# A transformer layer on one core: attention weights formed with the keys on partitions

## The chip, the cores and the metric

The kernel runs on one core of a Trainium2 chip. The metric is the device time in microseconds (us). Before the change it was 1210.74 us, the median of three runs (1210.34 to 1212.61). The engines are PE (TensorE, matrix products), DVE (VectorE), ACT (ScalarE) and POOL (GpSimd); SP is the queue that issues nearly all the loads.

## The reference

One layer over 256 latent tokens and 256 context tokens of width 1024:

```python
mod = jnp.split((silu_c @ w_ada[l] + b_ada[l])[:, None, :], 6, axis=-1)
h = modulate(rms_norm(x, g_mix_pre[l]), mod[0], mod[1])      # and hc from ctx
y, yc = token_mixing(h, hc, ...)        # attention, then @ w_o
x = x + mod[2] * rms_norm(y, g_mix_post[l])
h2 = modulate(rms_norm(x, g_ffn_pre[l]), mod[3], mod[4])
f = moe_ffn(h2, ...)                    # top 4 of 32 experts, swiglu
x = x + mod[5] * rms_norm(f, g_ffn_post[l])
```

`token_mixing` has two groups of eight heads. The first (GQA, heads of 64, two key heads) reads all context keys and the latent keys within 128 positions; its softmax has one more logit per head, the sink, which adds to the sum and has no value. The second (MLA) has queries and keys of 96 (64 and 32) and values of 64, formed by two further projections. Each softmax runs over 512 keys, and the 16 head outputs of 64 columns are multiplied by `w_o`.

## The kernel before

Everything that must be exact to fp32 is computed on PE in one of two ways: natively (an fp32 product), or as `mm3` (L137 to L139): both operands are split into a high and a low part of the type fp32r (L128 copies the high part on ACT, L129 subtracts on DVE or POOL), and three fp32r products are added in PSUM.

The program has three parts. First, up to about 98 us, the modulation rows, the norms and the projections into `qTg`, `kTg`, `vg` (GQA) and the latent vectors (MLA). Second, attention: 16 heads go through a loop of 19 steps. In step u head u gets its scores for the two query tiles (`scores`: an `mm3` of 128 queries by 512 keys, for GQA a mask product, then the row maximum on DVE at L614, the negated maximum at L616 or L619, the exponential with its row sum on ACT at L628, the sink's term at L634, the reciprocal at L636 and the scaling of the weights at L637, on POOL for query tile 0 and on DVE for 1). Head u-2 gets its weights transposed, 128 by 128 at a time (`flip_p`, L646), and split; head u-3 its values (`values`, L656: high and low parts of the values lie side by side in 128 columns, so the result is two halves that are added at L669). Two heads make one of eight blocks of the output product, `mix` (L677 natively for blocks 0 to 3, `mm3` for 4 to 7, with the weights `wo` split into two parts).

Between these steps stand jobs that don't belong to attention: `k_up`, `q_up`, `v_up` form the MLA keys, queries and values; `ada_load` loads four modulation rows, 1 MB for every quarter of a row, into buffers of a ring (`slot`), and `ada_do` multiplies and adds each quarter with two DVE instructions on 128x1024 (L427; two of the rows have every second one on ACT and POOL, L424 and L425). The last row goes into `vpost`. `spread1` and `column` bring the rows into the shape in which they are used.

Third, from `mix(7)` on: `y` is normed, the router picks experts, and 32 experts are computed from 384 loads of 1 MB each (`wexp`, L744), 18 buffers in turn: eight of the ring, six that are free once attention is over, four of a second ring. L926 are the experts' products.

A scheduler sets the order of PE, DVE, ACT and POOL up to `mix(7)`; on SP the order is that of the program, as it is for all engines afterwards. Each engine executes its list strictly in order.

Of the kernel before, what the change touches and what calls it, by code (L numbers as in the profile page):

```python
# [69 lines left out]
WOU = (3, 6, 9, 12)  # L70
# [3 lines left out]
def layer_kernel(ctx, tc, x, cx, cc, wadr, bada, grows, win0, winB, winC, winD, wuqa, wuqb, wukv, wo, wr, wexp, bgu, bgx, bdn, cols, rows, consts, out):  # L74
# [7 lines left out]
    def slot():  # L82
        return ring.tile([P, 2048], F32, name="slot", tag="slot")

# [89 lines left out]
    pq.tile([P, 512], F32, name="p", tag="pb")  # L174
# [151 lines left out]
    def halves(n):  # L326
        r = slot().bitcast(F32R)
        return [r[:, i * n:(i + 1) * n] for i in range(2048 // n)]

    ckvT = [x_.rearrange("p (i k c) -> p i k c", k=2, c=P) for x_ in halves(1024)]  # L330
    kv_ = slot().bitcast(F32R)
    kTg = [kv_[:, 0:512], kv_[:, 512:1024]]
    vg = kv_[:, 1024:2048].rearrange("p (i h c) -> p i h c", h=2, c=P)
    qTg = [x_.rearrange("p (t j c) -> p t j c", t=NT, c=P) for x_ in halves(1024)]
# [39 lines left out]
    def stage_b(i, p_):  # L374
        t = i - 2
        pv = p_[:, 128:256].rearrange("p (h d) -> p h d", h=2)
        S.copy(vg[:, i, :, 0:64], pv)
        V.tensor_tensor(vg[:, i, :, 64:128], pv, vg.bitcast(F32)[:, i, :, 0:64], op=ALU.subtract)
# [99 lines left out]
    vm = av.tile([P, 4, 8, P], F32R, name="vm")  # L478
    nsink = sm.tile([P, 8], F32, name="nsink", bufs=1)
    V.tensor_scalar(nsink, row[:, 0, R_SINK:R_SINK + 8], -1.0, None, op0=ALU.mult)  # L480
    pslot = slot()
# [37 lines left out]
    def v_up(i):  # L519
        pv = up(i, prow(), wv).rearrange("p (h d) -> p h d", h=8)  # L520
        S.copy(vm[:, i, :, 0:64], pv)
        V.tensor_tensor(vm[:, i, :, 64:128], pv, vm.bitcast(F32)[:, i, :, 0:64], op=ALU.subtract)

    prep = {0: [(k_up, 0), (k_up, 1)], 1: [(k_up, 2), (k_up, 3)], 2: [(q_up, 0, 0), (q_up, 0, 1)],
            3: [(v_split,), (q_up, 1, 0), (q_up, 1, 1)], 4: [(v_up, 0), (v_up, 1)], 5: [(v_up, 2), (v_up, 3)]}
# [10 lines left out]
    wos = {}  # L536

    def load_wo(i):
        wos[i] = slot()
        nc.sync.dma_start(wos[i], wo[i])  # L540

    def split_wo(i, qs):
        w = wos[i]
        if i in NATWO:
            for k in range(2):
                wov[2 * i + k] = w[:, k * 1024:(k + 1) * 1024]
            return
        if qs[0] == 0:
            wos[i, 0] = slot().bitcast(F32R), slot().bitcast(F32R)
        hi, lo = wos[i, 0]  # L550
        for q in qs:
            sl = slice(q * 512, (q + 1) * 512)
            split(hi[:, sl], lo[:, sl], w[:, sl], eng=G if q % 2 else V)
        for k in range(2):
            wov[2 * i + k] = [x_[:, k * 1024:(k + 1) * 1024] for x_ in (hi, lo)]
# [8 lines left out]
    def spread0(ch):  # L564
        gs_[ch] = gs, hl = slot(), slot().bitcast(F32R)
        q = 0 if ch == 0 else 1
        S.dma_start(gs[:, 0:D], bass.AP(tensor=grows.tensor, offset=grows.offset + q * D, ap=[[0, P], [1, D]]))
        for q in range(2):
            sl = slice(q * 512, (q + 1) * 512)
            split(hl[:, sl], hl[:, D + q * 512:D + (q + 1) * 512], accs[ch][:, sl], eng=G)  # L570

    def spread1(ch):
        a, (gs, hl) = accs[ch], gs_[ch]
        for n in range(2):
            sl = slice(n * 512, (n + 1) * 512)
            p_ = pmm((P, 512))
            PE.matmul(p_, onesr, hl[:, sl], start=True, stop=False)
            PE.matmul(p_, onesr, hl[:, D + n * 512:D + (n + 1) * 512], start=False, stop=True)
# [104 lines left out]
    def side(u):  # L683
# [5 lines left out]
        if 0 <= u < 12:  # L689
            ada_do()  # L690
# [566 lines left out]
```

## Time and profile before

| | |
|---|---|
| median of three runs | 1210.74 us |
| the profiled execution's own time | 1209.01 us |
| its span, first to last instruction | 1207.2 us |
| PE busy | 1108.8 us (92%) |
| DVE, ACT, POOL busy | 339.1, 277.1, 152.2 us |
| granted TensorE clock, mean | 0.975 |
| chain that ended last, by engine | DMA 54%, PE 34%, DVE 8% |
| moved by DMA | 446.59 MB, 370 GB/s on average |

The chain that ended last is followed back from the last instruction; its shares say on what the end waited, not what was busy. A row "start, us, ... xN" is a stretch of N records of one kind. Matrix products overlap: the time that one takes from the next is the distance of their starts (the pitch), not the duration shown. A native fp32 product leaves two records, an fp32r product one.

### The profile page before, as it was taken

To read this page: it belongs to the slowest core of one execution; us is meant where nothing else is said; L and a number is where in the kernel's file an instruction comes from. 1 tells how busy PE (TensorE), PEld (TensorE's weight loads), DVE (VectorE), ACT (ScalarE), POOL (GpSimd) and SP (SyncE) were. 2 spreads that over 40 slices of the span, in tenths; PEclk is the share of its full clock that TensorE was granted. 3 is DMA by queue.
4 is the path that set the end of the run, shared out by engine and by line. 5 is a ranking of instruction groups with operands and counts; after the bars stand their busy time and mean duration, and the time that the engine had idled before them with its cause. 6 is when DMAs were issued, how large, how long until landed. Compare 5 with 4: busy or idle time off the path is not lost.

```text
span 1207.2 us, 13663 instructions
## 1 busy us (share of the span) xinstructions
PE 1108.8 (92%) x5321; PEld 484.0 (40%) x5321; DVE 339.1 (28%) x778; ACT 277.1 (23%) x623; POOL 152.2 (13%) x182
## 2 busy tenths in 40 slices
PE   7798888999999999999989899989899999999985
PEld 1596556863433434343333333333333333333321
DVE  3867997752111111111111111111111111111112
ACT  4445654641111111111101111111111111111101
POOL 0503533310011010101010000000000101010000
PEclk9999879999999999999999999999999999999998
DMA  9534461699999999999999999999999999999994
GB/s 381 223 149 175 150 252 53 258 412 422 376 421 421 420 420 420 420 420 421 421 420 420 421 420 420 421 420 420 420 420 421 422 420 420 421 420 421 421 422 172
DMA packets 63196, 446.59 MB, mean 370 GB/s; under 512 B 7284, under 2 KB 7540, under 8 KB 10008
## 3 DMA queue, kind: packets, MB, share of 16 engines
q1 hardware_dynamic: 62648, 444.23, 89.4%
q10 hardware_dynamic: 480, 1.44, 0.3%
q8 instruction: 44, 0.72, 0.2%
q14 instruction: 24, 0.20, 0.0%
HBM read 444.60 MB, written 1.05 MB: 369 GB/s over the span
## 4 chain that ended last, share of the span: by engine, by line
DMA 54%; PE 34%; DVE 8%; ACT 1%; issue 1%; POOL 0%; SPq 0%; POOLq 0%; DVEq 0%; ACTq 0%
DMA slot<-in_wexp 53%; PE pw L926 19%; PE px L891 2%; PE mm L267 2%; PE acc L956 2%; DVE accw L427 1%; PE mm L137 1%; PE y L677 1%; PE pf L939 1%; PE mm L139 1%; PE mm L138 1%; PE mm L656 1%; DVE mx L614 1%; PE mm L646 1%; DVE accw L314 1%
## 5 line engine op out<-in xcount | busy, mean ns | idle before, releaser
L926 PE MATMUL pw<-slot,xg 128*64 128x512 f32 x2048 | 468.0, 598 | 19.3 <-DMA slot<-in_wexp 19.2
L926 PE MATMUL pw<-slot,actT 128*64 128x512 f32 x1024 | 242.8, 600 | 28.3 <-DMA slot<-in_wexp 26.9
L926 PEld LDWEIGHTS pw<-slot,xg 128*64 128x64 f32 x2048 | 136.5, 136 | 302.5 <-issue 233.2
L944 DVE TENSOR_TENSOR z<-pf,bg 128x512 f32<-128x512 f32 x64 | 44.3, 692 | 754.3 <-PE pf L939 754.3
L926 PEld LDWEIGHTS pw<-slot,actT 128*64 128x64 f32 x1024 | 68.6, 136 | 178.5 <-issue 101.5
L948 ACT ACTIVATE sg<-z 128x256 f32<-128x256 f32 x64 | 26.6, 416 | 311.2 <-DVE z L946 311.2
L933 ACT COPY gu<-pw 128x512 f32<-128x512 f32 x64 | 37.5, 586 | 229.6 <-PE pw L926 229.6
L891 PEld LDWEIGHTS px<-oh,xt 128*128 128x128 f32 x480 | 57.5, 196 | 23.9 <-issue 23.9
L903 ACT ACTIVATE xg<-px,vcol 128x128 f32<-128x128 f32 x120 | 45.2, 457 | 92.4 <-PE px L891 92.4
L956 PE MATMUL acc<-y,ctt 64*128 64x512 f32 x256 | 63.6, 615 | 0.7 <-ACT y L933 0.7
L891 PE MATMUL px<-oh,xt 128*128 128x128 f32 x480 | 63.3, 286 | 0.3 <-DVE cnt L1011 0.3
L939 PEld LDWEIGHTS pf<-con,gu 128*128 128x128 f32 x256 | 26.8, 140 | 52.7 <-issue 51.1
L939 PE MATMUL pf<-con,gu 128*128 128x128 f32 x256 | 42.0, 286 | 0.7 <-ACT gu L933 0.7
L933 ACT COPY y<-pw 128x512 f32<-128x512 f32 x32 | 18.8, 586 | 91.0 <-PE pw L926 91.0
L637 POOL TENSOR_SCALAR p<-p,su 128x512 f32<-128x512 f32 x16 | 28.2, 1760 | 52.3 <-DVE su L636 29.9
L881 POOL TENSOR_SCALAR oh<-con,posm,r 128x64 f32<-128x64 f32 x60 | 34.1, 585 | 2.5 <-DVE posm L821 2.5
L950 DVE TENSOR_TENSOR sg<-z,sg 128x256 f32<-128x256 f32 x64 | 27.2, 426 | 18.0 <-ACT sg L948 18.0
L956 PEld LDWEIGHTS acc<-y,ctt 64*128 64x128 f32 x256 | 22.0, 186 | 21.8 <-issue 18.4
L115 POOL TENSOR_TENSOR rstd<-rstd,mh 128x1 f32<-128x1 f32 x14 | 10.3, 733 | 146.2 <-DVE rstd L112 130.2
L951 DVE SCALAR_TENSOR_TENSOR actT<-z,sg 128x256 f32<-128x256 f32 x64 | 27.2, 425 | 2.2
L267 PE MATMUL mm<-slot,siluz 128*4 128x512 f32 x40 | 20.6, 669 | 7.3 <-DMA slot<-in_wadr 7.3
L918 ACT COPY ctt<-px 128x256 f32<-128x256 f32 x32 | 12.0, 375 | 62.2 <-PE px L917 62.2
(466 smaller groups left out, 1029.6 us busy)
## 6 DMA issues: line engine op xcount, KB each, us to landing
slot<-in_wexp SPq DMA_DIRECT2D x384, 1024.0 KB, 19.8
slot<-in_wadr SPq DMA_DIRECT2D x20, 1024.0 KB, 6.5
ax<-in_wadr SPq DMA_DIRECT2D x4, 1024.0 KB, 5.2
slot<-in_wo SPq DMA_DIRECT2D x4, 1024.0 KB, 5.4
slot<-in_win SPq DMA_DIRECT2D x2, 1024.0 KB, 7.9
slot<-in_winD SPq DMA_DIRECT2D x2, 768.0 KB, 11.5
slot<-in_winB SPq DMA_DIRECT2D x2, 576.0 KB, 9.5
ct<-in_cx SPq DMA_DIRECT2D x2, 512.0 KB, 13.1
```

What stands on the lines that cost most here:

```text
L267: PE.matmul(pad[ch][n], siluz[:, 2 * s + k], w[:, k, n * 512:(n + 1) * 512], start=(s == 0 and k == 0), stop=(last and k == 1), skip_group ...
L637: (V if t else G).tensor_scalar(p, p, r, None, op0=ALU.mult)
L881: eng.tensor_scalar(oh[t][:, i], iota[:, 0:CAP], pos_ap(t), r2[t], op0=ALU.is_equal, op1=ALU.mult)
L891: PE.matmul(px[:, k, 0:ne * CAP], xt[t][:, kk * P:(kk + 1) * P], self.oh[t][:, 0:ne].rearrange("p e c -> p (e c)"), start=(k == 0 and t == ...
L903: S.activation(o, i, AF.Identity, scale=vcol[:, 1, kk:kk + 1], bias=vcol[:, 0, kk:kk + 1])
L926: PE.matmul(pt[HALF[h]], lhs(k), wk(k, h), start=(k == 0), stop=(k == KD - 1), skip_group_check=True)
L933: S.copy(y, pt)
L939: PE.transpose(pf[:, b].rearrange("p h c -> p (h c)"), gu[:, b * P:(b + 1) * P], ident)
L944: V.tensor_tensor(z, pf, bias[:, :, :, None].to_broadcast([P, 4, 2, CAP]), op=ALU.add)
L950: V.tensor_tensor(sg, zg, sg, op=ALU.mult)
L951: V.scalar_tensor_tensor(actT[:, 4 * c:4 * c + 4], zl, 1.0, sg, op0=ALU.add, op1=ALU.mult)
L956: PE.matmul(acc[t][n], ctt[HALF[n], t], y[HALF[n]], start=False, stop=last, skip_group_check=True)
```

## The change

The scores of the weights are formed transposed, with the keys on partitions, so that no weight is transposed afterwards. For this the row maximum must be known beforehand, and on partitions it can't be taken off by a bias; so:

- `top_a` and `top_b` form a one-pass product (high parts only) of 128 queries by 512 keys for every head and query tile and take its row maximum on DVE. `shift` negates the maxima (for GQA with the sink), transposes them (L613) and rounds them to fp32r as rows `nmax`.
- `weights(u)` works on a pair of heads: for each of four key tiles and each head three fp32r products of 256 queries, and a fourth that adds the row `nmax` by way of a selecting matrix `sel`; for GQA, mask products; then the exponential (ACT), straight into `pT`. POOL adds half the key tiles to the other half (`pa`).
- `values(u)` multiplies `pT` natively in fp32 with the values, the two heads side by side in the two halves of the columns; four products of `pa` with ones and, for GQA, two for the sink give the sums. DVE takes the reciprocal of 128x256 sums (L675) and multiplies (L677).
- `mix` is native for all eight blocks, `spread1` too; the splits of the weights, the values, `wo` and the modulation rows go.
- The ring has five buffers instead of eight; the three others are held for `ckvT`, `kTg` and `qTg`, and become buffers of `wexp` later (`RSEQ`: d0, d1, d2).

The core of the diff (`k_up` to `v_up`, the order of the calls, and the loads of `wo` change with it):

```diff
-R1 = 8
+R1 = 5
-RSEQ = ("r", "r", "k0", "q0", "r", "r", "r", "k1", "q1", "b0", "b1", "r", "r", "r", "x", "x", "x", "x")
+RSEQ = ("r", "r", "d0", "d1", "r", "r", "d2", "k0", "q0", "b0", "k1", "q1", "b1", "r", "x", "x", "x", "x")
...
+    def top_a(j):
+
+        if j == 0:
+            mxs["a"] = sm.tile([P, NT, 8], F32, name="mxa", bufs=1)
+        for t in range(NT):
+            s_ = [pmm((P, 512)) for h in range(2)]
+            for h in range(2):
+                PE.matmul(s_[h], qTg[0][HALF[h], t, j], kTg[0][HALF[h]], start=True, stop=False, skip_group_check=True)
+            kb = 3 - t
+            for h in range(2):
+                PE.matmul(s_[h][:, kb * P:(kb + 1) * P], ident_b, mask_b[:, t * P:(t + 1) * P], start=False, stop=True,
+                          skip_group_check=True)
+            for h in range(2):
+                V.tensor_reduce(mxs["a"][:, t, 4 * h + j:4 * h + j + 1], s_[h], axis=AX.X, op=ALU.max)
+
+    def top_b(h):
+        n, j = divmod(h, 4)
+        if j == 0:
+            mxs[n] = sm.tile([P, NT, 4], F32, name=f"mxb{n}", bufs=1)
+        for t in range(NT):
+            s_ = pmm((P, 512))
+            PE.matmul(s_, qTm[n][0:96, 0, t, j], kTm[0][n][0:96, j], start=True, stop=True)
+            V.tensor_reduce(mxs[n][:, t, j:j + 1], s_, axis=AX.X, op=ALU.max)
+
+    def shift(g):
+
+        m, n = mxs[g], 8 if g == "a" else 4
+        if g == "a":
+            V.scalar_tensor_tensor(m, m, -1.0, nsink[:, None].to_broadcast([P, NT, 8]), op0=ALU.mult, op1=ALU.min)
+        else:
+            V.tensor_scalar(m, m, -1.0, None, op0=ALU.mult)
+        p_ = pmm((P, T))
+        for t in range(NT):
+            PE.transpose(p_[0:n, t * P:(t + 1) * P], m[:, t], ident)
+        r = rows_[g] = av.tile([8, T], F32R, name="nmax", tag="nmax", bufs=2)
+        S.copy(r[0:n], p_[0:n])
+        if g == "a":
+            ess[g] = av.tile([8, T], F32, name="es", bufs=1)
+            S.activation(ess[g], r.bitcast(F32), AF.Exp, scale=A_SCALE, bias=col[0:8, G_SINK:G_SINK + 1])
+
+    pT_ = {}
+    pa_ = {}
+
+    def weights(u):
+
+        a = u < 4
+        pT_[u] = [av.tile([P, 4, T], F32, name="pT", bufs=4) for h in range(2)]
+        pa_[u] = [av.tile([P, 2, T], F32, name="pa", bufs=2) for h in range(2)]
+        for g in range(2):
+            st = [pmm((P, 2, T)) for h in range(2)]
+            for kk in range(2):
+                kt = 2 * g + kk
+                ks = slice(kt * P, (kt + 1) * P)
+                ops = []
+                for h in range(2):
+                    if a:
+                        k_ = [x_[HALF[h], ks] for x_ in kTg]
+                        q_ = [x_[HALF[h], :, u] for x_ in qTg]
+                        sl, r = sel[:, 4 * h + u], rows_["a"]
+                    else:
+                        n, j = divmod(2 * (u - 4) + h, 4)
+                        k_ = [x_[n][0:96, j, ks] for x_ in kTm]
+                        q_ = [qTm[n][0:96, i, :, j] for i in range(2)]
+                        sl, r = sel[0:4, j], rows_[n][0:4]
+                    ops.append([(k_[0], q_[0]), (k_[0], q_[1]), (k_[1], q_[0]), (sl, r)])
+                for i in range(4):
+                    for h in range(2):
+                        PE.matmul(st[h][:, kk], *ops[h][i], start=(kk == 0 and i == 0), stop=(i == 3 and not (a and g)),
+                                  skip_group_check=True)
+                if a and g:
+                    t = 3 - kt
+                    for h in range(2):
+                        PE.matmul(st[h][:, kk, t * P:(t + 1) * P], mask_b[:, t * P:(t + 1) * P], ident_b, start=False,
+                                  stop=True, skip_group_check=True)
+            for h in range(2):
+                S.activation(pT_[u][h][:, 2 * g:2 * g + 2], st[h], AF.Exp, scale=A_SCALE if a else B_SCALE)
+        for h in range(2):
+            G.tensor_tensor(pa_[u][h], pT_[u][h][:, 0:2], pT_[u][h][:, 2:4], op=ALU.add)
+
+    def values(u):
+        pT, pa = pT_.pop(u), pa_.pop(u)
+        po = pmm((P, 2, T))
+        for kt in range(4):
+            for h in range(2):
+                vs = vg[:, kt, h] if u < 4 else vm[:, kt, 2 * (u - 4) + h]
+                PE.matmul(po[HALF[h], 0], vs, pT[h][:, kt], start=(kt == 0), stop=(kt == 3), skip_group_check=True)
+        for i in range(2):
+            for h in range(2):
+                PE.matmul(po[HALF[h], 1], ones_f[:, 0:64], pa[h][:, i], start=False, stop=(i == 1 and u >= 4),
+                          skip_group_check=True)
+        if u < 4:
+            for h in range(2):
+                PE.matmul(po[HALF[h], 1], sel.bitcast(F32)[:, 4 * h + u, 0:64], ess["a"], start=False, stop=True,
+                          skip_group_check=True)
+        rz = av.tile([P, T], F32, name="rz", bufs=2)
+        V.reciprocal(rz, po[:, 1])
+        oT[u] = av.tile([P, T], F32, name="of", bufs=OFB)
+        V.tensor_tensor(oT[u], po[:, 0], rz, op=ALU.mult)
+
+    def mix(k):
+        for t in range(NT):
+            for n in range(2):
+                PE.matmul(y[t][n], oT[k][:, t * P:(t + 1) * P], wov[k][:, n * 512:(n + 1) * 512],
+                          start=(k == 0), stop=(k == KD - 1), skip_group_check=True)
+
...
+    for i in range(4):
+        top_a(i)
+        k_up(i)
+        ada(1)
+    shift("a")
+    for n in range(2):
+        for t in range(NT):
+            q_up(n, t)
+        if n == 0:
+            v_split()
+            ada(1)
+    for i in range(4):
+        v_up(i)
+    open_y()
+    spread0(0)
+    load_wo(0)
+    for j in range(4):
+        weights(j)
+        top_b(2 * j)
+        top_b(2 * j + 1)
+        if j % 2:
+            shift(j // 2)
+        if j:
+            values(j - 1)
+        if j > 1:
+            mix(j - 2)
+        if j == 0:
+            spread1(0)
+            load_wo(1)
+            column(1)
+        ada(2)
+    for u in range(4, 8):
+        weights(u)
+        values(u - 1)
+        mix(u - 2)
+        if u < 6:
+            load_wo(u - 2)
+        if u == 4:
+            column(2)
+            ada(2)
+            spread0(3)
+        if u == 6:
+            spread1(3)
+    values(7)
+    mix(6)
```

Three places of the instruction lists. The first is SP, the loads between the projections and the experts. Before (L414 and L411 load the modulation rows, L540 `wo`):

```order
L411 DMA accw_109<-in_bada 1x1024
L414 DMA slot<-in_wadr 128x2048
L540 DMA slot<-in_wo 128x2048
L414 DMA slot<-in_wadr 128x2048 x3
L540 DMA slot<-in_wo 128x2048
L411 DMA vpost<-in_bada 1x1024
L414 DMA slot<-in_wadr 128x2048 x3
L540 DMA slot<-in_wo 128x2048
L414 DMA slot<-in_wadr 128x2048
L540 DMA slot<-in_wo 128x2048
L744 DMA slot<-in_wexp 128x2048 x2
```

And of the changed kernel (L412, L409 and L534 are the same loads, L760 the experts'):

```order
L409 DMA accw_109<-in_bada 1x1024
L412 DMA slot<-in_wadr 128x2048 x3
L534 DMA slot<-in_wo 128x2048 x2
L412 DMA slot<-in_wadr 128x2048
L409 DMA vpost<-in_bada 1x1024
L412 DMA slot<-in_wadr 128x2048 x4
L534 DMA slot<-in_wo 128x2048 x2
L760 DMA slot<-in_wexp 128x2048 x2
```

The last modulation row's four loads (into `vpost`) now stand in one piece, behind two loads of `wo`.

The second is DVE, where the last modulation row is added up. Before (L614 is a row maximum, L616 its negation, L129 the low part of a split, L635 and L636 the sum and its reciprocal):

```order
L427 SCALAR_TENSOR_TENSOR vpost<-slot,silu,vpost 128x1024
L614 TENSOR_REDUCE mx<-mm 128x1
L427 SCALAR_TENSOR_TENSOR vpost<-slot,silu,vpost 128x1024
L616 SCALAR_TENSOR_TENSOR nm<-mx,nsink 128x1
L129 TENSOR_TENSOR pTl<-mm,pTh 128x4x128
L614 TENSOR_REDUCE mx<-mm 128x1
L427 SCALAR_TENSOR_TENSOR vpost<-slot,silu,vpost 128x1024
L635 TENSOR_TENSOR su<-su,es 128x1
L616 SCALAR_TENSOR_TENSOR nm<-mx,nsink 128x1
```

And of the changed kernel (L425 is the same addition, L602 a row maximum of MLA heads, L610 its negation, L675 and L677 the normalisation of the values; L565, L566 and L570 belong to `column(1)`):

```order
L602 TENSOR_REDUCE mxb_1319<-mm 128x1 x4
L425 SCALAR_TENSOR_TENSOR accw_109<-slot,silu,accw_109 128x1024
L556 TENSOR_TENSOR accw_107<-mm,slot 128x512 x2
L565 COPY vcol<-mm 128x8
L425 SCALAR_TENSOR_TENSOR vpost<-slot,silu,vpost 128x1024
L566 TENSOR_TENSOR accw_108<-wrs,vcol 128x256
L425 SCALAR_TENSOR_TENSOR vpost<-slot,silu,vpost 128x1024 x2
L570 TENSOR_TENSOR rb<-mm,row 128x32
L425 SCALAR_TENSOR_TENSOR vpost<-slot,silu,vpost 128x1024 x5
L602 TENSOR_REDUCE mxb_1319<-mm 128x1 x4
L610 TENSOR_SCALAR mxb_1319<-mxb_1319 128x8
L675 RECIPROCAL rz<-mm 128x256
```

All eight additions now stand ahead of the second four row maxima of the first MLA group, where before row maxima stood between them.

The third is PE, at the first values of attention. Before (L677 is `mix`, L656 the values, L584 and L592 `column`, L137 to L139 and L610 scores and their mask, L646 transposes):

```order
L677 MATMUL y_1581<-slot,of 128x512
L656 MATMUL mm<-pTh,slot 128x256 x4
L656 MATMUL mm<-pTl,slot 128x256 x4
L584 MATMUL mm<-con,accw_108 128x1 x8
L592 MATMUL mm<-accw_108,con 128x32 x8
L137 MATMUL mm<-slot 128x512
```

And of the changed kernel (L647 are score products, of which those with `nmax` add the shift; L601 is the one-pass product for maxima, L613 transposes the maxima, L665, L668 and L672 are the values and their sums):

```order
L647 MATMUL mm<-slot_397,slot_396 128x256 x5
L647 MATMUL mm<-nmax,sel 128x256 x2
...
L601 MATMUL mm<-kTm_958,qTm_962 128x512 x4
L613 MATMUL mm<-con,mxb_1319 4x128 x2
L665 MATMUL mm<-pT,vg 64x256 x8
L668 MATMUL mm<-pa,con 64x256 x4
L672 MATMUL mm<-es,sel 64x256 x2
L647 MATMUL mm<-slot_397,slot_396 128x256 x6
L647 MATMUL mm<-nmax,sel 128x256 x2
```

The transposes of the MLA maxima stand ahead of the first values; up to here PE has done the scores of two pairs of heads, and no values and no `mix`.

## Rows read from the trace of the kernel before

**Rows 1.** the chain that ended last: start, us, what (its last load)
```profile
1170.55 19.76 DMA slot<-in_wexp
```

**Rows 2.** windows: PE, PEld, DVE, ACT, POOL busy us (records), clock, DMA share, GB/s
```profile
98.00:133.00 35.00, 27.11 (x122) 17.86 (x121) 30.47 (x60) 22.82 (x54) 20.43 (x11) 0.85 0.25 91
133.00:165.00 32.00, 26.93 (x142) 18.63 (x141) 30.89 (x62) 18.79 (x41) 14.81 (x7) 0.97 0.69 262
165.00:182.00 17.00, 17.00 (x55) 11.82 (x56) 16.33 (x25) 7.10 (x17) 4.02 (x4) 0.50 0.51 189
195.00:244.00 49.00, 46.88 (x260) 36.07 (x260) 35.51 (x87) 27.05 (x64) 14.33 (x9) 1.00 0.52 203
...
262.00:305.00 43.00, 40.57 (x173) 15.48 (x172) 12.63 (x44) 7.22 (x16) 1.19 (x2) 0.90 1.02 415
...
315.00:320.00 5.00, 5.00 (x26) 1.69 (x24) 0.00 (x0) 0.59 (x1) 0.00 (x0) 1.00 0.67 249
```

**Rows 3.** timeline of PE: last product of y, first of the experts
```profile
245.98 0.39 PE L139 MATMUL y<-slot 128*128 128x512 f32 x1
...
262.28 1.08 PE L926 MATMUL pw<-slot,xg 128*64 128x512 f32 x4
```

**Rows 4.** timeline of SP's queue: start, us, issue
```profile
153.54 12.67 SPq L414 DMA_DIRECT2D slot<-in_wadr  x3
...
218.94 2.54 SPq L744 DMA_DIRECT2D slot<-in_wexp  x4
```

**Rows 5.** timeline of DVE, 146 to 150 us
```profile
146.21 1.27 DVE L427 SCALAR_TENSOR_TENSOR accw<-slot,silu,accw 128x1024 f32<-128x1024 f32 x1
147.40 0.68 DVE L522 TENSOR_TENSOR vm<-pr,vm 128x512 fp32r<-128x512 f32 x1
148.00 0.68 DVE L129 TENSOR_TENSOR pTl<-mm,pTh 128x512 fp32r<-128x512 f32 x1
...
149.20 1.85 DVE L616 SCALAR_TENSOR_TENSOR nm<-mx,nsink 128x1 f32<-128x1 f32 x1
```

**Rows 6.** timeline of POOL, the same stretch
```profile
148.65 2.38 POOL L425 TENSOR_TENSOR accw<-accw,slot 128x1024 f32<-128x1024 f32 x1 [4.15 <-ACT slot L424]
```

**Rows 7.** groups by line, 97 to 260 us: busy, mean ns, idle before
```profile
L637 POOL TENSOR_SCALAR p<-p,su 128x512 f32<-128x512 f32 x16 | 28.2, 1760 | 52.3 <-DVE su L636 29.9 <-DVE su L635 11.7 <-DVE nm L619 7.7
L129 DVE TENSOR_TENSOR pTl<-mm,pTh 128x512 fp32r<-128x512 f32 x32 | 21.7, 682 | 3.1 <-ACT pTh L128 2.9
```

**Rows 8.** loads by line, from the page: issue to landing last
```profile
slot<-in_wadr SPq DMA_DIRECT2D x20, 1024.0 KB, 6.5
```

**Rows 9.** timeline of PE: pitches, in time order, five stretches
```profile
143.29 0.50 PE L137 MATMUL mm<-slot 64*128 64x512 f32 x1
143.63 0.39 PE L138 MATMUL mm<-slot 64*128 64x512 f32 x1
143.86 0.39 PE L139 MATMUL mm<-slot 64*128 64x512 f32 x1
...
186.04 0.63 PE L656 MATMUL mm<-pTl,slot 128*128 128x256 f32 x4
186.51 0.40 PE L137 MATMUL mm<-kTm,qTm 96*128 96x512 f32 x1
...
208.99 3.70 PE L677 MATMUL y<-slot,of 128*128 128x512 f32 x8 [0.35 <-DVE of L669]
212.53 0.60 PE L646 MATMUL mm<-con,p 128*128 128x128 f32 x4
...
336.95 1.99 PE L956 MATMUL acc<-y,ctt 64*128 64x512 f32 x8
338.87 7.09 PE L926 MATMUL pw<-slot,xg 128*64 128x512 f32 x32
345.89 0.33 PE L939 MATMUL pf<-con,gu 128*128 128x128 f32 x1
```

**Rows 10.** timeline of DVE: a reciprocal of 16 columns
```profile
2.83 0.25 DVE L180 RECIPROCAL ex<-ex 128x16 f32<-128x16 f32 x1
```

More of the change, by code (lines that the diff above doesn't have):

```diff
@@ L324, in layer_kernel, with halves @@
     wB = kview(load1(winB[0], 1152, "a", True) + load1(winB[1], 1152, "b", True, G), 288)
[L326 to L327 removed]
+    def halves(n, i):
+        r = held(i).bitcast(F32R)
         return [r[:, i * n:(i + 1) * n] for i in range(2048 // n)]
[L330 to L331 removed]
+    ckvT = [x_.rearrange("p (i k c) -> p i k c", k=2, c=P) for x_ in halves(1024, 0)]
+    kv_ = held(1).bitcast(F32R)
     kTg = [kv_[:, 0:512], kv_[:, 512:1024]]
[L333 to L334 removed]
+    qTg = [x_.rearrange("p (t j c) -> p t j c", t=NT, c=P) for x_ in halves(1024, 2)]
     def proj(w, ws, n):
@@ L520, in v_up @@
         pv = up(i, prow(), wv).rearrange("p (h d) -> p h d", h=8)
[L521 to L525, printed above, removed]
+        S.copy(vm[:, i], pv)
     y = []
@@ L534, in layer_kernel @@
     oT = {}
-    wos = {}
     def load_wo(i):
[L539 to L553, printed above, removed]
+        w = slot()
+        nc.sync.dma_start(w, wo[i])
         for k in range(2):
-            wov[2 * i + k] = [x_[:, k * 1024:(k + 1) * 1024] for x_ in (hi, lo)]
+            wov[2 * i + k] = w[:, k * 1024:(k + 1) * 1024]
     vmix = accs[0]
@@ L564, in spread0 @@
     def spread0(ch):
[L565 to L570, printed above, removed]
+        gs_[ch] = slot()
+        S.dma_start(gs_[ch][:, 0:D], bass.AP(tensor=grows.tensor, offset=grows.offset + (0 if ch == 0 else 1) * D,
+                                             ap=[[0, P], [1, D]]))
     def spread1(ch):
-        a, (gs, hl) = accs[ch], gs_[ch]
+        a, gs = accs[ch], gs_[ch]
         for n in range(2):
@@ L702, in layer_kernel, with ada @@
+    def ada(n):
+        for _ in range(n):
+            if ada_n[0] < 16:
+                ada_load()
+            if ada_q:
+                ada_do()
     ada_load()
     ada_load()
-    mk_ = 0
-    for u in range(16 + 3):
-        for t in range(NT):
-            if u < 16:
-                scores(u, t)
-            if 0 <= u - 2 < 16:
-                flip_p(u - 2, t)
-        if u >= 3:
-            values(u - 3)
-        for f in prep.get(u, ()):
-            f[0](*f[1:])
-        if u == 6:
-            open_y()
-        if u >= 6:
-            for _ in range(2):
-                if mk_ < KD - 1 and (mk_ < (u - 3 + 1) // 2 and (u - 3) % 2 or mk_ < (u - 3) // 2):
-                    mix(mk_)
-                    mk_ += 1
-        side(u)
+    for i in range(4):
+        top_a(i)
+        k_up(i)
+        ada(1)
@@ L1192, in _layout @@
     w["wuqb"] = np.concatenate([uq[2], kv[:, 1024:2048]], 1)
-    w["wo"] = g["w_o"].reshape(4, 2, P, D).transpose(0, 2, 1, 3).reshape(4, P, 2048)
+    o_ = g["w_o"].reshape(16, 64, D)[HEADS_A + list(range(8, 16))]
+    w["wo"] = o_.reshape(4, 2, P, D).transpose(0, 2, 1, 3).reshape(4, P, 2048)
     w["wr"] = g["w_router"].reshape(KD, P, E).transpose(1, 0, 2)
@@ L1205, in _layout @@
     w["cols"] = np.concatenate(
-        [g[n].reshape(-1, P).T for n in ("b_ada", "g_mix_pre", "g_q_a", "g_kv_a", "g_ffn_pre")], 1)
+        [g[n].reshape(-1, P).T for n in ("b_ada", "g_mix_pre", "g_q_a", "g_kv_a", "g_ffn_pre")]
+        + [np.tile(g["sink"].reshape(8, 1), (P // 8, 1))], 1)
     pos = np.arange(T)
```

123 lines of the change are left out of this document (17 added, 106 removed).

## The prediction, made before the changed kernel ran

> **What bounds the kernel now.** I read the chain that ended last first. It ends on a load of the experts' stream that took 19.76 us from issue to landing [rows 1]: with 18 buffers in flight each load queues behind others. In the windows the stream runs at 415 GB/s [rows 2], so a load of 1.05 MB takes 2.5 us, and the 384 loads 970 us. It starts at 218.94 us [rows 4], and PE's first expert product at 262.28 [rows 3]: 43 us, some 17 loads, so the buffers are nearly full when PE starts. Soon afterwards the stream stalls for lack of free buffers: 249 GB/s between 315 and 320 instead of 415 [rows 2], 2 us lost. From there on it is full. So the end of the kernel stands where the experts start, give or take these 2 us, and they start 16 us after the last product of y (245.98 with its 0.2 us, call it 246.2 [rows 3]). The routing in between is not changed. What the change is worth is therefore read from one time: when y is done.
>
> What limits y changes along the way. Between 98 and 165 us DVE is busy 61 of 67 us while PE has gaps of 13; from 195 to 244 PE is busy 46.88 of 49 and DVE 35.51 [rows 2]. So DVE limits the first half, PE the second, and in between PE works 17 us without a gap at a clock of 0.50, the lower of its two levels [rows 2].
>
> **What goes.** DVE loses the low parts of the transposed weights (21.7 us in 32 [rows 7]), half the scaling, the 1-column sums and reciprocals, the low parts of values and weights `wo`; POOL loses 28.2 us of scaling [rows 7] and gets 16 additions of 128x512. Some DVE time goes twice over, because a one-column instruction at 149.20 took 1.85 us [rows 5]; it ended at 151.05, with POOL's addition that ran from 148.65 for 2.38 [rows 6]. PE loses 128 transposes and the half of the mix that was three products.
>
> **What comes, in three stretches.**
>
> *From 98.7 to the last GQA maximum.* Nothing of attention's weights can start before all 16 GQA maxima are there, and DVE's list up to them holds, by the order of instructions, 28 instructions of 128x512 (16 maxima, 7 key splits, 5 of the query path), 5 ada additions and one split of 128x1024, two scalings of 128x384 and some small ones. The pitch of a 128x512 is 0.60 us and of a 128x1024 1.19 (147.40 to 148.00, 146.21 to 147.40) [rows 5]. 28 x 0.60 + 6 x 1.19 + 2 is 26 us. In this stretch DVE had 4.5 idle us of 35 before [rows 2], and POOL's locks come on top; I add 8 and put the shift at 133. Bounds: 130 and 137.
>
> *From the shift to the first values.* PE has the rest of `q_up`, 24 `v_up` products at 0.23 (143.63 to 143.86) [rows 9], and the first scores: about 14 us, to 147. The first values stand on PE behind the transposes of the first MLA maxima (the third place of the order), those behind DVE's second four maxima, and those behind all eight additions of the last modulation row (the second place). SP issues its four loads in a row (the first place), into buffers that the last `v_up` and the additions set free. So the first of them goes out about 147, the others 2.5 us apart, and one lands 6.5 us after its issue [rows 8]: 147 + 7.5 + 6.5 = 161. Two additions (2.4), four maxima (2.4) and the transposes: 166. Before, three of these loads went out from 153.54 on [rows 4] too, but nothing on PE waited for them. What is queued behind the wait on PE is everything, from the values of pair 0 to the last mix; on hand it has only the scores of pairs 0 and 1, `column(1)`, `spread1(0)` and four maxima products, about 13 us, so 6 of the 19 are idle. Bounds for the first values: 150 if the loads are early (then PE's own work counts), 172 if the slot of the fourth waits for the first's additions.
>
> *From the first values to y.* Now PE is alone. `mix`: a block of four native products takes 3.54 us (208.99 to 212.53) [rows 9], eight of them 28.3. Values: a native product of 512 columns is 0.885, of 256 0.44. L926, whose products use 64 columns, does 16 (32 records) in 7.02 us [rows 9], that is 0.44 for 512 columns, half of it: two halves of the columns go side by side. So a pair's 12 products (14 with the sink) take 2.65 (3.1), together 23.0. Scores of an MLA pair: 32 fp32r products of 256 queries at 0.12 (four in 0.47, 186.04 to 186.51 [rows 9]) are 3.8. Scores of a GQA pair work on 64 rows; L956, on 64 rows, does four native products of 512 in 1.92 us, so 0.48 [rows 9], and two halves of the rows go side by side too: 24 at 0.06, eight of the shift at 0.12 and four masks make 2.6. The first product of another shape costs more: 0.34 at 143.29 against 0.23 behind it [rows 9], so 0.11 for a change between 64, 96, 4 or 128 rows. At six to eight such changes a pair I take 3.5 for a GQA pair and 4.5 for MLA: 2 x 3.5 + 4 x 4.5 = 25. Eight maxima products 1.9, `spread1(3)` 1.8, `column(2)` 1. Sum 81. On top, waits that nothing covers: the second `shift` 1.5; at the end values(7), then DVE's reciprocal and product, then mix(7), with only mix(6) for cover. The reciprocal: 16 columns take 0.25 us [rows 10]; if nearly half of that is a start, 256 take 1.75, with the product 2.2 us after the last sum, 2.4 with the hand-over; its bounds are 0.3, the pitch of other instructions of that size [rows 5], and 4, if the 0.25 scales. POOL's two additions for a pair (no such row; a scaling of the same size took 1.76 [rows 7]; 1 to 2.4 each) stand behind the exponentials and ahead of the products with ones; a mix or another pair's scores, 3.5 us, lie beside them, and without that cover a pair costs up to 3.5. The exponentials, four of 128x512 a pair as before, lie beside PE. I add 5 for other waits and a lower clock at the start. 81 + 1.5 + 2.4 + 5 = 90, so y at 256, 10 us later than 246.2. Bounds of this stretch: 77 (no change of shape costs anything, no other wait) and 100.
>
> On the change of shape the Trainium skill speaks against this kernel: TensorEngine Tiling (Array Packing), section Key Properties, has a change of the tiling mode drain the engine. The 0.11 of the 64-row scores agrees with it; without the rule the sum would be about 4.6 us lower, and a longer drain is part of the third rival.
>
> On the reciprocal, VectorE: DVE Perf Modes, section Terms, in the Trainium skill, names an iterated division with a repeat count of 8. An estimate from that and its clock of 0.96 GHz is 2.1 us for 256 columns, 0.4 more at the end than the 1.75 from the row.
>
> The ring of five in place of eight only matters early, where the loads are the limit anyway; the first weights' loads wait for one another, not for buffers. I cost it at nothing; if that cover is gone, each late load costs up to 2.5 us. The experts' loads start as `mix` sets slots free, so again some 17 are in when PE gets there. Up to 2 us of the stall at 315 can be given back; I count 1.
>
> Sum: 1209.0 (the profiled execution) + 10 - 1 = 1218; the median is 1.7 above that execution, so 1220.
>
> **The rivals.**
> 1. *Faster: the relief of DVE counts.* If the four loads of the last row are early, the first values go at 150, and PE, with no wait left, needs 81 + 9: y at 240, 6 us early, 1204. For it: DVE is the limit up to 165 and loses the most. Against: the order of the loads. It decides if PE's gap ahead of the first values is under 5 us. 0.17.
> 2. *No change.* The gap is 10 us and the last stretch close to its 77 with few waits: 160 + 85 = 245, 1209 to 1213. 0.13.
> 3. *Slower still.* After gaps like those of the first stretch PE works at the lower clock, as at 165 to 182 [rows 2], for 17 us or more: 8 us; or the halves don't go side by side in short runs of mixed shapes, 0.06 for each of 48 score products, 3 us, and a part of the 23 us that the values would double by, 8 to 12 us in all. y at 264 to 268, 1228 to 1232. This needs PE to be the engine that is waited for, as it is from 166 on. 0.20.
> 4. *The change doesn't do what it says* (the maxima wait for the old chain): excluded by the order, in which no transpose of weights is left.
>
> **How the numbers follow.** My forecast of 1220 has 0.50. A measurement of this kernel can tell 0.2%, 2.4 us, from no change. Slower by more than that holds the forecast and rival 3, 0.70; faster 0.17; the same 0.13. The range reaches from the middle of rival 2's side, 1207, to 1232; the likeliest case's own is 1214 to 1227.
>
> **What would show it.** In the changed kernel's profile: PE idle around 155 to 166, ended by L613 or values that wait for DVE's L602; DVE in front of it waiting for loads of the modulation rows; `nmax` of GQA at 130 to 137; from there PE over 90% busy; `mix` 3.5 us a block; the reciprocal near 1.75 us; y done near 256, and the experts 16 us later. I am wrong if the values start by 155, if a pair of values takes 5 us, or if the end does not move with y.

## The result and the profile after

The changed kernel takes 1260.86 us (median of four runs, 1260.24 to 1263.55) against 1210.95 for the kernel before beside it: a ratio of 1.041, interval [1.040, 1.043]. The direction was forecast, the size was not: 50 us slower, where 1220 us (9 slower) stood, with a range to 1232.

The end still follows y, as the prediction had it. The timeline of PE, the last block of `mix` and the first expert product (L940) of the changed kernel, which answer to [rows 3]:

```profile
293.10 5.40 PE L682 MATMUL y<-slot,of 128*128 128x512 f32 x8 [2.31 <-DVE of L677]
...
313.95 10.52 PE L940 MATMUL pw<-slot,xg 128*64 128x512 f32 x48
```

y is done at 298.3 instead of 246.2, 52.1 us later; the experts start 51.7 us later; the span grew from 1207.2 to 1259.3, by 52.1. So the loss lies ahead of y. The windows of the changed kernel, for [rows 2] (PE, PEld, DVE, ACT, POOL busy us; clock; DMA share; GB/s), with the stretch from the first values to the end of y last:

```profile
98.00:133.00 35.00, 28.68 (x104) 15.86 (x102) 28.12 (x39) 16.87 (x31) 13.80 (x8) 0.80 0.45 164
133.00:165.00 32.00, 29.18 (x144) 21.25 (x144) 18.44 (x40) 10.25 (x19) 5.83 (x3) 0.83 0.49 183
165.00:182.00 17.00, 15.55 (x78) 9.54 (x78) 9.23 (x10) 2.53 (x5) 2.10 (x2) 0.61 0.50 183
195.00:244.00 49.00, 47.28 (x218) 28.70 (x215) 10.24 (x14) 7.09 (x13) 7.49 (x6) 0.82 0.07 22
...
175.85:298.50 122.65, 118.62 (x505) 66.66 (x505) 26.29 (x34) 16.46 (x32) 18.03 (x15) 0.81 0.22 89
```

DVE is relieved (10.24 us of 49 where it had 35.51), and it does not help: PE is busy nearly throughout, and the stretch from the first values to y is longer than forecast (122.65 us where 90 stood). Its mean granted clock is 0.81; from 195 to 244 it is 0.82 where the same window before had 1.00 [rows 2]. Smaller windows of the changed kernel show where the clock goes; the scores of MLA pairs are at 233.39 and 250.05, each followed by a mix, and the values at 260.61:

```profile
233.39:240.96 7.57, 7.57 (x33) 5.68 (x33) 0.59 (x2) 1.27 (x3) 0.00 (x0) 0.68 0.01 2
240.96:247.31 6.35, 6.35 (x10) 2.49 (x12) 0.00 (x0) 0.90 (x2) 0.00 (x0) 0.57 0.00 0
...
250.05:256.14 6.09, 6.09 (x33) 4.51 (x33) 2.18 (x2) 1.68 (x3) 2.51 (x2) 1.00 1.01 429
256.14:260.61 4.47, 4.47 (x8) 1.60 (x10) 0.00 (x0) 0.60 (x1) 0.00 (x0) 0.62 0.05 18
260.61:263.35 2.74, 2.74 (x25) 1.63 (x25) 0.00 (x0) 0.00 (x0) 0.00 (x0) 1.00 0.03 6
```

Two things are to be seen. The scores at 250.05 ran at 1.00 throughout and still took 6.09 us, where 4.5 was forecast. And the mix behind scores is at 0.57 to 0.62, part of the time at the lower of the two levels, though its products are the native ones that were forecast at 3.5 us a block; during the values the clock is back at 1.00. The timeline of PE inside the scores (`nmax` marks the shift product on 4 rows; L647 without it the products on 96 rows):

```profile
252.64 0.50 PE L647 MATMUL mm<-qTm,kTm 96*128 96x256 f32 x2
252.98 0.28 PE L647 MATMUL mm<-qTm,kTl 96*128 96x256 f32 x1
253.19 0.38 PE L647 MATMUL mm<-nmax,sel 4*128 4x256 f32 x1
253.50 0.50 PE L647 MATMUL mm<-qTm,kTm 96*128 96x256 f32 x2
```

Four products of 0.12 would be 0.48 us; from 252.64 to 253.50 it is 0.86. The one short product brings 0.38 us on top, two changes of shape at 0.19.

### The profile page after: what moved, and what is told of

The parts are those of the page before. It is cut to its first block, busy times and chain, and to the rows that moved or that the text cites. A ratio compares the mean times of both kernels' runs of the same rounds, so it can differ in the third digit from the quotient of the medians.

```text
span 1259.3 us, 13672 instructions
## 1 busy us (share of the span) xinstructions
PE 1165.2 (93%) x5471; PEld 502.3 (40%) x5471; DVE 297.0 (24%) x637; ACT 241.3 (19%) x516; POOL 134.1 (11%) x174
## 4 chain that ended last, share of the span: by engine, by line
DMA 52%; PE 40%; DVE 5%; issue 1%; ACT 1%; POOL 0%; SPq 0%; POOLq 0%; ACTq 0%; DVEq 0%
DMA slot<-in_wexp 51%; PE pw L940 18%; PE mm L647 4%; PE y L682 3%; PE px L907 2%; PE mm L267 1%; PE acc L970 1%; PE mm L665 1%; DMA slot<-in_wadr 1%; PE pr L501 1%; PE pf L953 1%; DVE accw L425 1%; PE mm L668 1%; PE mm L137 1%; PE mm L138 1%
## 5 line engine op out<-in xcount | busy, mean ns | idle before, releaser
L940 PE MATMUL pw<-slot,xg 128*64 128x512 f32 x2048 | 468.5, 599 | 18.8 <-DMA slot<-in_wexp 18.8
L940 PE MATMUL pw<-slot,actT 128*64 128x512 f32 x1024 | 242.8, 601 | 28.9 <-DMA slot<-in_wexp 27.7
L940 PEld LDWEIGHTS pw<-slot,xg 128*64 128x64 f32 x2048 | 136.7, 137 | 302.2 <-issue 233.0
L940 PEld LDWEIGHTS pw<-slot,actT 128*64 128x64 f32 x1024 | 68.6, 136 | 179.4 <-issue 99.8
L682 PE MATMUL y<-slot,of 128*128 128x512 f32 x64 | 44.0, 836 | 2.3 <-DVE of L677 2.3
L655 ACT ACTIVATE pT<-mm 128x512 f32<-128x512 f32 x32 | 18.0, 595 | 97.7 <-PE mm L647 75.4
L657 POOL TENSOR_TENSOR pa<-pT 128x512 f32<-128x512 f32 x16 | 20.9, 1328 | 110.0 <-PE mm L668 110.0
L964 DVE TENSOR_TENSOR sg<-z,sg 128x256 f32<-128x256 f32 x64 | 27.2, 425 | 18.1 <-ACT sg L962 18.1
L675 DVE RECIPROCAL rz<-mm 128x256 f32<-128x256 f32 x8 | 14.1, 1758 | 71.3 <-PE mm L668 48.9
```

Of the source, the lines that this page charges most:

```text
L682: PE.matmul(y[t][n], oT[k][:, t * P:(t + 1) * P], wov[k][:, n * 512:(n + 1) * 512], start=(k == 0), stop=(k == KD - 1), skip_group_check=True)
L940: PE.matmul(pt[HALF[h]], lhs(k), wk(k, h), start=(k == 0), stop=(k == KD - 1), skip_group_check=True)
L964: V.tensor_tensor(sg, zg, sg, op=ALU.mult)
```

## The experiments

The diffs show only the lines that decide. "By the ratios" means that each kernel is compared with the kernel before beside it, which took 1209.7 to 1213.5 us. Theory A: the short shift products (8 or 4 rows between products on 64 or 96) make the scores slow and, behind them, the clock low. Theory B: the clock falls for another reason, and the short products cost only themselves.

**Without the shift products:**

```diff
-ops.append([(k_[0], q_[0]), (k_[0], q_[1]), (k_[1], q_[0]), (sl, r)])
+ops.append([(k_[0], q_[0]), (k_[0], q_[1]), (k_[1], q_[0])])
```

> The eight products per pair that add the shift row (8 or 4 rows) are left out, so the exponentials are those of unshifted scores. Theory A: these short products cost PE twice, by the change between 64 or 96 rows and 8 or 4 rows at each, and by the lower clock that follows the scores. Then a pair's scores take 2.2 to 3.2 us instead of 6 to 8, the mix returns to 3.5 us a block at clock 1.00, and the time is 1212 to 1222 us. Theory B: the clock falls for another reason (native products of 64 columns, or the 256-query products themselves); then the scores lose only the eight products, the mix stays at 5 to 6 us a block, and the time is about 1238.

Measured: 1219.71 us, 1.008 of before [1.005, 1.010]. The group of the mix and the window from the first values to y:

```profile
L682 PE MATMUL y<-slot,of 128*128 128x512 f32 x64 | 29.6, 600 | 2.5 <-DVE of L677 2.5
```
```profile
169.10:255.30 86.20, 81.76 (x457) 48.43 (x457) 26.28 (x34) 16.25 (x32) 17.95 (x15) 0.97 0.36 143
```

This kernel leaves out the shift. 64 products less (7.7 us at 0.12) brought 41 us. The mix is back at 29.6 us for its eight blocks (44.0 in the changed kernel). Theory A, not B.

**The same products on full rows.** The maxima are padded with zeros before their transpose, so that the shift has 64 rows for GQA and 96 for MLA:

```diff
-sl, r = sel[:, 4 * h + u], rows_["a"]
+sl, r = sel[HALF[h], 4 * h + u], rows_["a"][HALF[h]]
...
-sl, r = sel[0:4, j], rows_[n][0:4]
+sl, r = sel[0:96, j], rows_[n][0:96]
```

> The same eight shift products, but on as many rows as the score products beside them (64 in the matching half for GQA, 96 for MLA; the added rows are zero), so that the number of products stays and the change of shape goes. Theory A: a pair's scores take 3.3 to 4.5 us, the clock stays at 1.00 in the mix, 1220 to 1230 us. Theory B: 1240 to 1250, with the mix still at 5 to 6 us a block. If the number of products alone counts, 1260.

Measured: 1227.35 us, 1.013 of before [1.010, 1.016]. Windows of the last stretch and of one MLA pair's scores, and the mix:

```profile
173.60:268.20 94.60, 90.57 (x504) 56.79 (x505) 26.17 (x34) 16.33 (x32) 17.99 (x15) 0.92 0.28 111
...
233.03:237.03 4.00, 4.00 (x34) 4.00 (x34) 2.18 (x2) 1.60 (x3) 2.53 (x2) 1.00 1.01 426
```
```profile
L689 PE MATMUL y<-slot,of 128*128 128x512 f32 x64 | 30.2, 602 | 2.3 <-DVE of L684 2.3
```

As many products, the same sums, 33.5 us less by the medians. (The trace is of an execution of 1231.54 us, 4 above the median.) A pair's scores fall from 6.09 to 4.00 at equal clock, and the clock of the stretch rises from 0.81 to 0.92.

Not every stretch at the lower level belongs to the short products. Here the scores behind `column(2)`, whose 16 products have 1 column, ran at 0.52 with no short product among them. In the run with the late row below, the scores behind the same products ran at 1.00; the two windows:

```profile
219.90:226.70 6.80, 6.80 (x34) 6.80 (x35) 0.59 (x2) 1.08 (x2) 0.00 (x0) 0.52 0.00 1
```
```profile
213.40:217.50 4.10, 4.10 (x37) 4.10 (x37) 0.59 (x2) 1.08 (x2) 0.00 (x0) 1.00 0.02 6
```

In the changed kernel the scores at 233.39 stand behind `column(2)` too, so their 0.68 can't be put down to the short products alone.

**Half as many changes.** The four shift products of two key tiles stand together behind the twelve others:

```diff
-for i in range(4):
+for i in range(3):
...
+for kk in range(2):
+    for h in range(2):
+        PE.matmul(st[h][:, kk], *late[kk][h][3], start=False, ...)
```

> The four shift products of two key tiles stand together behind their twelve score products, so there are half as many changes of shape, with the same products. Theory A: half of the effect of full rows, about 1240 to 1247 us. Theory B: 1252 to 1258, and the mix keeps its clock.

Measured: 1242.59 us, 1.026 [1.022, 1.029]. Between the two, as A had it; the mix too, and an MLA pair's scores at clock 1.00, which now have 6 changes of shape:

```profile
240.79:245.73 4.94, 4.94 (x33) 4.14 (x33) 2.18 (x2) 1.68 (x3) 2.53 (x2) 1.00 1.00 421
```
```profile
L688 PE MATMUL y<-slot,of 128*128 128x512 f32 x64 | 39.4, 757 | 2.3 <-DVE of L683 2.3
```

**Twice the short products**, adjacent, at half their size each:

```diff
-(k_[1], q_[0]), (sl, r)])
+(k_[1], q_[0]), (sl, r), (sl, r)])
```

> The changed kernel with every short shift product issued twice at half its size (64 more of 8 or 4 rows in all, the sum is the same), the pairs mostly adjacent. Theory A: what costs is the change of shape and what follows at the clock, so adjacent second products add little more than their 0.11 to 0.2 us each, 8 to 13 us, and the clock falls no further: 1266 to 1276 us. If each short product brings its own drain and lowers the clock further: 1280 or more.

Measured: 1269.84 us, 1.046 [1.043, 1.048]: inside the expected 1266 to 1276; over the changed kernel it is 9 us by the medians and 5 by the ratios, for 64 products 0.08 to 0.14 each. The last stretch:

```profile
177.50:305.40 127.90, 126.14 (x552) 75.62 (x552) 26.20 (x33) 16.25 (x32) 17.84 (x15) 0.78 0.19 73
```

So in the direct cost theory A holds: four short products in a row take 0.67 us (182.59 to 183.26) where two in the changed kernel take 0.43 (180.79 to 181.22), so a second one beside the first costs no more than its columns, 0.12, and what costs is the change. In the clock it doesn't: that the clock falls no further was expected, and its mean went from 0.81 to 0.78. Nor is the number of changes the same. Counted in the traces, the last stretch has about 66 changes to and from shift products here, 76 in the changed kernel, 44 in the grouped one and 8 with full rows. With fewer changes and twice the short products the clock is lower.

**Which change.** Shift products on 128 rows for both groups (the diff is against full rows):

```diff
-sl, r = sel[HALF[h], 4 * h + u], rows_["a"][HALF[h]]
+sl, r = sel[:, 4 * h + u], rows_["a"]
-sl, r = sel[0:96, j], rows_[n][0:96]
+sl, r = sel[:, j], rows_[n]
```

> As full rows, but every shift product on 128 rows, so GQA changes between 64 and 128 rows and MLA between 96 and 128. Theory S: a change between tile sizes of the array costs, and 64 to 128 is one while 96 to 128 is not. Then a GQA pair's scores cost as much as with 8 rows (5.4 us at clock 1.00 in place of 4.2), an MLA pair's stay at 4.0 to 4.3, and the time is 1230 to 1240 us. Theory R: any change of the number of rows costs, so both rise and the time is over 1245. Theory F: it is the few rows that cost, so neither rises and the time stays at 1225 to 1229.

Measured: 1234.91 us, 1.020 [1.019, 1.022]: theory S. The timeline of PE, first two shift products of a GQA pair, then those of an MLA pair:

```profile
179.46 0.62 PE L654 MATMUL mm<-slot,slot 64*128 64x256 f32 x6
180.01 0.50 PE L654 MATMUL mm<-nmax,sel 128*128 128x256 f32 x2
180.45 0.62 PE L654 MATMUL mm<-slot,slot 64*128 64x256 f32 x6
...
213.09 0.40 PE L654 MATMUL mm<-qTm,kTl 96*128 96x256 f32 x2
213.33 0.40 PE L654 MATMUL mm<-nmax,sel 128*128 128x256 f32 x2
213.56 0.63 PE L654 MATMUL mm<-qTm,kTm 96*128 96x256 f32 x4
```

The two products on 128 rows between others on 64 take 0.44 us, between others on 96 they take 0.23, which is 0.12 each. The products ahead of a change pay as well: from 179.46 to 180.45 it is 0.99 us, where six products on 64 rows (0.36 in the full-rows trace) and two at 0.12 make 0.60; so 0.39 for the two changes, 0.19 each. So in the direct cost it is neither few rows nor any other number of rows that counts, but a step between the kinds 8 or 4, 64, and 96 or 128. The Trainium skill (TensorEngine Tiling (Array Packing), Key Properties) has a change of mode drain the engine; the trace agrees, and a change costs 0.16 to 0.19 us here. A GQA pair's scores take 6.40 us at clock 1.00 where 5.4 was expected (first window below).

The clock is another matter. The second GQA pair's scores behind the first values, here and in the changed kernel:

```profile
194.50:200.90 6.40, 6.40 (x39) 4.70 (x37) 2.18 (x2) 1.68 (x3) 2.19 (x2) 1.00 0.01 3
```
```profile
197.22:205.16 7.94, 7.94 (x38) 5.48 (x38) 2.18 (x2) 1.68 (x3) 2.09 (x2) 0.80 0.01 2
```

With 13 changes between 64 and 128 rows in this pair (17 between 64, 8 and 128 in the changed kernel) the clock stays at 1.00, and so it does in the mix behind it (1.00 against 0.67). In the first such pair it fell here too (0.93 against 0.84), and the mean of the last stretch is 0.93, no lower than with full rows. So the changes alone don't explain the lower level. That the few rows have a part in it is likely by this, but not shown.

**The mix alone.** The kernel before with all blocks native:

```diff
-NATWO = {0, 1}
+NATWO = {0, 1, 2, 3}
```

> The kernel before with all eight blocks of the mix native, as in the changed kernel, and nothing else. Theory A: a native block costs 3.54 us at clock 1.00 against 2.8 for twelve fp32r products, so 3 us more on PE at most and less on DVE, 1209 to 1214 us. Theory B (native products bring the clock down): the mix takes over 4.5 us a block and the time is 1220 or more.

Measured: 1210.47 us, ratio 1.000 [0.998, 1.002]. A native mix costs nothing that can be measured there:

```profile
L677 PE MATMUL y<-slot,of 128*128 128x512 f32 x64 | 31.4, 635 | 1.4 <-DVE of L669 1.4
```

**The last modulation row.** The prediction had the first values wait for its loads. In the changed kernel DVE's list reads:

```profile
158.04 1.28 DVE L425 SCALAR_TENSOR_TENSOR vpost<-slot,silu,vpost 128x1024 f32<-128x1024 f32 x1 [0.76 <-DMA slot<-in_wadr]
159.24 0.42 DVE L566 TENSOR_TENSOR accw<-wrs,vcol 128x256 f32<-128x256 f32 x1
...
172.53 2.48 DVE L602 TENSOR_REDUCE mxb<-mm 128x1 f32<-128x512 f32 x4 [1.98 <-PE mm L601]
```

The maxima waited for PE in the end, not for loads; but `column(1)` (L566) stood behind an addition that did, and PE idled for it ahead of L569. With full rows, where PE is quicker, the chain of waits shows the forecast wait itself:

```profile
160.12 7.42 DMA slot<-in_wadr
167.63 1.29 DVE vpost L425
168.95 1.28 DVE vpost L425
170.24 2.40 DVE mxb L606 x4
172.90 0.69 PE mm L620 x2
173.59 3.61 PE mm L672 x16
```

Two runs move the row's loads behind all loads of `wo`, with full rows and without:

```diff
-        ada(2)
+        if j == 0:
+            ada_load()
+        if j < 3:
+            ada_do()
...
+        if u in (5, 6):
+            ada_load()
+            ada_load()
```

> Full rows as in the run before, and the last modulation row's four loads moved behind all loads of wo, so that most of its additions come after the second four MLA maxima. Theory A2: the first values waited for these loads (they started at 173.6 us in the full-rows run, behind additions that waited for loads at 152.3 and 160.1). Then they start near 160 to 164, y is done near 256 and the time is 1214 to 1219 us. Theory B2: PE's own list sets the first values; then they move by under 4 us and the time is 1223 to 1228. If the late loads hold back the experts' loads, DMA waits show at the experts' start and the time is over 1228.

> The changed kernel with only the last modulation row moved, short shift products as they were. Theory A2: with the short products the scores of the second pair ran at the lower clock until 171.6 us and hid most of the wait for the loads, so the first values move by 3 us or less from 175.8, 1256 to 1260 us. If the wait for the loads is worth as much here as with full rows: about 1250.

Measured: with full rows 1221.85 us, 1.008 [1.005, 1.010], by the ratios 6 us better than full rows alone, with intervals that touch, and between the two theories: the first values came at 167.9 instead of 173.6. Without full rows 1253.49 us, 1.033 [1.031, 1.035], 10 us better by the ratios: my expectation of 3 us or less missed. The timelines of PE at L569, of the changed kernel and of this one:

```profile
159.72 3.62 PE L569 MATMUL mm<-accw,con 128*128 128x32 f32 x16 [2.65 <-DVE accw L566]
```
```profile
156.69 1.97 PE L569 MATMUL mm<-accw,con 128*128 128x32 f32 x16 [0.73 <-DVE accw L566]
```

I had looked for the wait at the maxima alone. It also stood ahead of `column(1)`, whose products then ran at the lower level. That is a part of the gain only: the first values came at 170.5 instead of 175.85, 5 us earlier, and the stretch from there to y took 118.1 us instead of 122.65. In it the wait of 2.31 us ahead of the last mix is gone; the other 2 us are not explained.

**Attempts at a better version**, all on top of full rows and the late row (the run with the late row: 1221.85 us, 1.008). DVE folds the sums once more:

```diff
+V.tensor_tensor(pa[h][:, 0], pa[h][:, 0], pa[h][:, 1], op=ALU.add)
```

> As the run with the late row, and DVE folds the POOL sums once more, so a pair has two products with ones instead of four (16 products of 0.22 us less on PE, 3.5 us). If PE alone sets the last stretch: 3 to 4 us below the run with the late row. If DVE's fold, which stands behind POOL's addition, is waited for: no gain or a loss of up to 5 us.

Measured: 1227.80 us, 1.012 [1.010, 1.013], 5 to 6 us worse. The first values came at 171.8, 4 us later, and the wait ahead of the last mix is back at 2.31 us. That the fold is waited for isn't shown by this: ahead of the first values an addition of the last modulation row, which waited for its load, stands in front of the negated maxima again (169.72 us).

The MLA shift as a 97th row of the score products, and then, on top of that, `column(1)` moved to the fifth pair:

```diff
-k_ = [x_[n][0:96, j, ks] for x_ in kTm]
-q_ = [qTm[n][0:96, i, :, j] for i in range(2)]
+k_ = [x_[n][0:97, j, ks] for x_ in kTm]
+q_ = [qTm[n][0:97, i, :, j] for i in range(2)]
```
```diff
-            column(1)
...
         if u == 4:
+            column(1)
             column(2)
```

> The late-row kernel, and for MLA the shift is a 97th row of the score products themselves (row of ones on the keys, the shift on the queries' high part), so their 32 shift products go and the transposes of the maxima are four times as many. If PE alone sets the last stretch: an MLA pair's scores 3.0 us in place of 3.8 to 4.0, 3 to 4 us less in all, 1217 to 1220 us by the runs of before of the late-row call. If the longer way to the shift is waited for: no gain.

> As the fold, and column(1) moved from ahead of the second pair's scores to the fifth pair. In the late-row run PE waited for DVE ahead of it at 150.7, and the second pair's scores ran at the lower clock behind it (5.9 us for 4.2). If that is what the small products of column(1) and the wait bring: the first values 5 to 8 us earlier, near 160, 3 to 7 us less than the fold. If the clock falls wherever column(1) stands: the loss moves along, and the time stays.

Measured: 1229.81 us, 1.016 [1.014, 1.018], and 1227.78, 1.013 [1.009, 1.018]. In the first an MLA pair's scores do fall (3.21 us for 24 products), but the scheduler put additions of the last modulation row ahead of the negated maxima again, and the first values came at 176.3; from its chain:

```profile
159.88 6.78 DMA slot<-in_wadr
...
169.32 4.88 DMA slot<-in_wadr
...
234.32 3.21 PE mm L665 x24
```

In the second the first values came 6 us earlier, at 170.0 (5 to 8 us, near 160, was expected), but the loss moved along with `column`: behind L569 and L577, products of 1 and 32 columns, the scores of a pair take 5.33 us instead of 3.2. The two times don't differ by more than their intervals; the second kernel's four runs lie between 1220 and 1231.

```profile
219.14 1.71 PE mm L577 x16
220.84 1.99 PE mm L569 x16
222.83 5.33 PE mm L665 x24
```

No version came below the kernel before.

## Why the prediction was wrong

*What bounds the kernel* held: the end moved by 52.1 us with y's 52.1, the experts' loads hid nothing of it. None of the three signs of being wrong that the prediction named came true; the step that failed had none.

*The first stretch* was right: the last GQA maxima are in the chain of the changed kernel at 131.22 and end at 132.4, where I had the shift at 133. *The second* was 10 us late: the first values came at 175.85, not 166, and later than the bound of 172. The wait for the loads was there, but at another place (`column(1)`), and the products of `column(1)` and the second pair's scores behind it ran at the lower level, 12.3 us at 0.50; by an estimate from that, some 6 of the 10 us. Chain and window:

```profile
131.22 1.20 DVE mxa L593 x2
```
```profile
163.30:172.00 8.70, 8.70 (x38) 6.23 (x38) 6.52 (x6) 1.20 (x3) 0.00 (x0) 0.50 0.87 306
```

*The last stretch* is the step that failed: 122.65 us instead of 90. The scores took 18.1 more (six pairs, 43.1 us in all, where 25 stood) and the mix 15.7 (44.0 for 28.3); the rest came out a little shorter. Values, reciprocal and uncovered waits were sized well: 2.74 us a pair (2.65 forecast), 1758 ns (1.75), 1.72 and 2.31 us (1.5 and 2.4):

```profile
L675 DVE RECIPROCAL rz<-mm 128x256 f32<-128x256 f32 x8 | 14.1, 1758 | 71.3 <-PE mm L668 48.9 <-PE mm L672 22.4
```

The 2.1 us that the prediction estimated for the reciprocal from the Trainium skill (VectorE: DVE Perf Modes; the repeat count stands there under "First, the fixed hardware budget") is too long; the measured 1.758 decides.

The first mis-sized term is "0.11 for a change between 64, 96, 4 or 128 rows", at six to eight changes a pair. It is 12 changes where the scheduler put the products of one head together, at 0.17 to 0.19 us: the 2.09 us between 6.09 and 4.00. And 96 to 128 rows is no change at all. The price stood in the trace of the kernel before and was read by half. This product stands ahead of the one at 143.29 [rows 9]:

```profile
142.97 0.39 PE L139 MATMUL pr<-slot 128*128 128x512 f32 x1
```

From 142.97 to 143.29 it is 0.32 us and from there to 143.63 it is 0.34, where a product takes 0.23: 0.09 ahead of the change and 0.11 behind it, 0.20 together. I counted the second half alone. Twelve changes at 0.17 are 2 us a pair and 12 in all, where I had under 5; the places could have been counted in the order.

The second is the clock. I allowed "5 for other waits and a lower clock at the start" and put an 8 us loss into a rival with 0.20. An estimate from the windows: a mean of 0.81 between levels of 1.0 and 0.5 is 38% of 122.65 us at the lower one, 23 us lost; with full rows 0.92 of 94.6 us, 8 lost. So the short products between others cost some 12 us directly (99 against 87 us at full clock) and some 16 through the clock. Rival 3 named PE at the lower level while it is what all wait for, but tied it to gaps of idle time. PE was not idle in these stretches: it was busy with short products between others.

That the change is what costs directly is shown by the pairs at clock 1.00: 4.00 us without changes, 4.94 with 6, 6.09 with 12. That the short products bring the lower level is shown by the kernels without them and with full rows (0.97 and 0.92 against 0.81). What in them does it is not shown. Half as many changes with the same products bring 0.86, twice the products with fewer changes 0.78, and changes between 64 and 128 rows leave 0.93: neither the number of changes nor that of the products alone puts these in order.

The rest of the loss, 9 us with full rows and the late row, is as large as the forecast. From 133 us to the end of y, PE had more to do than before and waited less; the kernel before and the run with the late row:

```profile
133.00:246.20 113.20, 103.66 (x513) 76.14 (x511) 93.45 (x198) 60.53 (x141) 40.00 (x23) 0.89 0.53 203
```
```profile
133.00:255.80 122.80, 118.59 (x675) 77.45 (x674) 50.68 (x78) 27.98 (x55) 24.82 (x18) 0.91 0.37 141
```

PE is busy 118.59 us where it was 103.66. DVE's relief, 43 us, can bring no more than PE's waits, which were 9.5. Rival 1 fell on the PE side in the main: with the loads moved (two additions still stood ahead of the second four maxima), the first values came at 167.9, not 150, and the time was still 1.008 of before.

## What to carry to other kernels

Count the changes between products on up to 8, 64, and 96 or 128 rows in the order in which PE executes them, and price each at 0.2 us, however small the product. When a price is read from pitches, read the one ahead of the change as well as the one behind it. Pad a small operand with zero rows to the size of its neighbours, which here made the same sums 33 us cheaper, by the estimate above more than half of it through the clock. Where PE becomes the engine that all wait for, read its granted clock behind each kind of work before carrying a price over: a native mix cost 3.5 us a block behind transposes and 5.5 behind these scores. An engine relieved is worth no more than the waits on it of the engine whose list sets the end.

## What the runs showed of the hardware

Two halves of 64 columns do go side by side in short runs (16 records of values, eight products of 256 columns, in 1.88 us at clock 1.00; one after the other at 0.44 they would be 3.5). A change of the kind of rows costs 0.16 to 0.20 us, about half of it ahead of the first product of the new kind; 96 to 128 rows costs nothing. The clock can be low during and behind work in which PE is busy without a gap: 0.68 and 0.57 in windows that are 100% busy. In six of the eight windows of values of the changed kernel it was at 1.00 again.
